# A fifth Strassen pair in the second FFN product, and a reordering of the vector work around it

## The chip, the cores and the metric

The kernel runs on one core of one Trainium2 chip. The metric is device time in microseconds (us) of one execution. Three runs of the kernel before took 1232.46, 1233.25 and 1234.97 us, so the median is 1233.25 us.

The engines are named as in the profile: PE multiplies matrices (PEld is its weight load), DVE is the vector engine, ACT the scalar engine, POOL GpSimd, and SP issues most of the DMAs. Each engine takes its instructions strictly in the order in which the program lists them for that engine; a waiting instruction holds up everything listed behind it.

## The reference, cut to what matters

The model is a two-layer trunk on 256 tokens of width 1024. Each layer is an FFN, a token mixer and a second FFN, so there are four FFN blocks in the program, and each ends in a layer norm:

```python
def _swiglu(x, w1, w3, w2):
    return (jax.nn.silu(x @ w1) * (x @ w3)) @ w2
...
for l in range(DEPTH):
    h = _swiglu(x, ffn_w1[l, 0], ffn_w3[l, 0], ffn_w2[l, 0])
    x = _layernorm(ALPHA * x + 0.5 * h, ln_g[l, 0], ln_b[l, 0])
    h = _mixer(x, l, ...)
    x = _layernorm(ALPHA * x + h, ln_g[l, 1], ln_b[l, 1])
    h = _swiglu(x, ffn_w1[l, 1], ffn_w3[l, 1], ffn_w2[l, 1])
    x = _layernorm(ALPHA * x + 0.5 * h, ln_g[l, 2], ln_b[l, 2])
```

The hidden width is 2816, so the second product `h @ w2` of each block sums over 22 slices of 128, which the kernel takes as 11 pairs of slices. Everything is float32.

## The kernel before, in words

**Split products.** PE multiplies in a reduced float32 format, so each float32 operand is cut into a high part and a low part. ACT writes the high part (a copy that rounds), then DVE writes the low part (raw minus high). One product of two blocks is three matmuls (`three`, L211): high by high, then low weight by high, then high weight by low. So the second of the three is the first that needs DVE's low split.

**Weights.** All weights stream through SBUF. A raw tile is 128 x 2048 (1 MB, one DMA from SP) out of a pool of 4; each half of it gets a high and a low tile of 128 x 1024, from pools of 8 each. `stream` (L159 to L174) does this for ordinary weights: names `raw`, `whi`, `wlo`.

**The second FFN product** (from L638 in `ffn`) is where the change lies. Eight PSUM banks of 128 x 512 hold 2 token halves t by 2 column halves c, in two sets.

- A *Strassen pair* (`SQ`, `stream_s`, names `raw`, `shi`, `slo`) multiplies its 2 x 2 blocks with seven products instead of eight: 7 x 3 = 21 matmuls of 128x512. The seven go to the banks S1 to S7 in the order 1, 2, 5, 6, 3, 7, 4. For the weight sums DVE adds in place in the raw tile (L309 over 1024 columns, L311 and L312 over 512 each). The four pieces to be split are `a` (512 columns, product 1), `b` (products 3 and 2), `c` (5 and 7, after the first sum) and `d` (6 and 4, after all sums). Two Strassen pairs share one tile for their `a` pieces. On the other side, `mixed` (L573) makes the sums of the activations: three small DVE instructions and one more split.
- A *plain pair* (`PQ`, `plain_pair`) is 8 x 3 = 24 matmuls.

The order in each block is: Strassen pair 0, plain pair, Strassen pair 1, plain pair, Strassen pair 2, plain pair, Strassen pair 3, and then four plain pairs that are *held*: they are split first, and then for each (t, c) the 24 matmuls of all four run into one bank, (0,0) first, so that the norm can start on one quarter while PE works on the next. The banks that only Strassen pairs use (S1, S5, S6, S7) close with the last Strassen pair and are added into the residual `x_tok` by eight vector instructions, the *folds* (L479, L667, L668, L477), with one ACT copy (L664). The remaining banks are added by `ln.part` (L486) when their held pairs are done.

**What sets the order.** PE's order is as written. The other engines' order is worked out at build time by a scheduler from the written order, a priority per streamed chunk and its own guess of times. `behind(x)` only forbids an instruction to stand ahead of `x`. The result is fixed before the kernel runs. How the pools give out buffers is fixed then too: a split into a high tile waits until PE has read what was in it.

Of the kernel before, what the change touches and what calls it, by code (L numbers as in the profile page):

```python
# [17 lines left out]
ALU = mybir.AluOpType  # L18
# [10 lines left out]
FB = 4  # L29
NB = 5  # L30
FR = NB * FB
NS = 4
SQ = [(FB + 2 * p, FB + 2 * p + 1) for p in range(NS)]
PQ = [(k, k + 1) for k in (0, 2, *range(FB + 2 * NS, FT, 2))]
HEADS = 8
# [21 lines left out]
def trunk(ctx, tc, x, xT, w13a, w13b, w2s, w2p, wb, wqk, wa, wbr, wo, gateb, sgug, sgub, sguwT, sgubias, lam, diffg,  # L57
          lng, lnb, lngT, lnbT, cosT, sinT, out):
    nc = tc.nc
    V, A, G, PE = nc.vector, nc.scalar, nc.gpsimd, nc.tensor  # L60
# [15 lines left out]
    def name(s):  # L76
        serial[0] += 1
        return f"{s}_{serial[0]}"
# [32 lines left out]
    def step():  # L111
        chunk[0] += 1
        tc.cur_priority = chunk[0] * STEP
# [12 lines left out]
    def beat(w):  # L126

        clock[0] += w
        for task in list(tasks):
            if task[0] <= clock[0]:  # L130
                turn(task)
# [15 lines left out]
    latest, added, emptied, silu, turned_by = [None, None], [None], [None], [None], [None]  # L147

    def behind(ins):

        return tc.issue_after(ins) if ins is not None else nullcontext()

    def stream(src, width=CH, sub=HC, lent=(), after=(None, None)):

        step()
        raw = raw_pool.tile([P, CH], F32, tag="raw", name=name("raw"))
        nc.sync.dma_start(raw[:, :width], src)  # L159
        out = []  # L160
        for o in range(0, width, HC):
            if o // HC in lent:
                hi, lo = ([act.tile([P, 512], F32R, tag="slot", name=name(n)) for _ in range(2)] for n in ("lhi", "llo"))
                at = [(hi[j], lo[j]) for j in range(2)]
            else:
                hi = hi_pool.tile([P, HC], F32R, tag="hi", name=name("whi"))
                lo = lo_pool.tile([P, HC], F32R, tag="lo", name=name("wlo"))
                at = [(hi[:, p : p + sub], lo[:, p : p + sub]) for p in range(0, HC, sub)]
            for p, (h, w) in zip(range(0, HC, sub), at):
                r = raw[:, o + p : o + p + sub]  # L170
                with behind(latest[0]):
                    A.activation(h, r, AF.Copy)  # L172
                with behind(after[o // HC] or latest[1]):
                    V.tensor_tensor(out=w, in0=r, in1=h.bitcast(F32), op=ALU.subtract)  # L174
            out.append((hi, lo))
        return out
# [34 lines left out]
    def three(ps, xh, xl, w_hi, w_lo, start, stop):  # L211

        for n, (w, xx) in enumerate([(w_hi, xh), (w_lo, xh), (w_hi, xl)]):
            PE.matmul(ps, xx, w, start=start and n == 0, stop=stop and n == 2)  # L214
# [40 lines left out]
    def rows_p(ps, t, q, piece, xh, xl, c0=0, n=512, stop=False, start=False):  # L255

        for j, k in enumerate(q):
            wh, wl = (v[:, j * 512 + c0 : j * 512 + c0 + n] for v in piece)
            three(ps[:, :n], xh(k)[:, t * P : (t + 1) * P], xl(k)[:, t * P : (t + 1) * P], wh, wl,
                  start and j == 0, stop and j == 1)  # L260
        beat(n / 1024)
# [21 lines left out]
    def stream_s(src, pair):  # L283

        step()
        raw = raw_pool.tile([P, CH], F32, tag="raw", name=name("raw"))
        nc.sync.dma_start(raw, src)

        def two():
            return hi_pool.tile([P, HC], F32R, tag="hi", name=name("shi")), lo_pool.tile([P, HC], F32R, tag="lo", name=name("slo"))  # L290

        def cut(p, o, n):
            h, w = (v[:, p[2] : p[2] + n] for v in p[:2])
            r = raw[:, o : o + n]
            with behind(latest[0]):
                A.activation(h, r, AF.Copy)  # L296
            with behind(latest[1]):
                V.tensor_tensor(out=w, in0=r, in1=h.bitcast(F32), op=ALU.subtract)  # L298

        a = (*pair, 0) if pair else None  # L300
        if a is None:
            pair = two()
            a, keep = (*pair, 0), pair
        else:
            a, keep = (*pair, 512), None
        b, c, d = ((*two(), 0) for _ in range(3))
        cut(a, 0, 512)
        cut(b, 1024, 1024)
        V.tensor_tensor(out=raw[:, :1024], in0=raw[:, :1024], in1=raw[:, 512:1536], op=ALU.add)  # L309
        cut(c, 0, 1024)  # L310
        V.tensor_tensor(out=raw[:, 1024:1536], in0=raw[:, :512], in1=raw[:, 1024:1536], op=ALU.add)  # L311
        V.tensor_tensor(out=raw[:, 1536:], in0=raw[:, 1024:1536], in1=raw[:, 1536:], op=ALU.add)  # L312
        cut(d, 1024, 1024)

        def at(p, j):
            return tuple(v[:, p[2] + j * 512 : p[2] + j * 512 + 512] for v in p[:2])

        return keep, {1: at(a, 0), 3: at(b, 0), 2: at(b, 1), 5: at(c, 0), 7: at(c, 1), 6: at(d, 0), 4: at(d, 1)}
# [246 lines left out]
    def ffn(l, f, i, norm, last=False):  # L565
# [77 lines left out]
        pair, held, plain = None, [], list(PQ)  # L643

        def plain_pair(hold):
            q = plain.pop(0)
            w = stream(w2p[l, f, PQ.index(q)])
            if hold:
                held.append((q, w))
                return  # L650
            for c in range(2):
                for t in range(NT):
                    for ps, o, m in ends[t, c]:
                        rows_p(ps, t, q, w[c], hh, hl, o, m, start=q == PQ[0] and t + c == 2)

        for n, q in enumerate(SQ):
            pair, w = stream_s(w2s[l, f, n], pair)
            for b in (1, 2, 5, 6, 3, 7, 4):
                three(S[b], *s_op[q][b], *w[b], n == 0, n == NS - 1 and b in (1, 5, 6, 7))
            beat(1.75)  # L660
            if n < NS - 1:
                plain_pair(False)
        u, v = s512("u"), s512("v")
        A.activation(u, S[6], AF.Copy)  # L664
# [2 lines left out]
        V.tensor_tensor(out=u, in0=u, in1=S[1], op=ALU.add)  # L667
        V.tensor_tensor(out=v, in0=S[5], in1=u, op=ALU.subtract)  # L668
        ln.more(0, 1, v, ALU.add, ln.scale)
        ln.more(1, 1, v, ALU.add, ln.scale)  # L670
        ln.more(1, 0, u, ALU.add)
        ln.more(1, 1, S[7], ALU.add)
        while plain:
            plain_pair(True)
        for t in range(NT):
            for c in range(2):
                for ps, o, n in ends[t, c]:
# [230 lines left out]
    for l in range(DEPTH):  # L908
        norm = ffn(l, 0, 0, norm)
        norm = mixer(l, 1, norm)  # L910
        norm = ffn(l, 1, 2, norm, last=l == DEPTH - 1)
# [89 lines left out]
```

## Time and profile before

| | |
|---|---|
| median of 3 runs | 1233.25 us |
| the profiled execution | 1233.15 us, of which its span is 1231.4 us |
| PE busy | 1215.8 us, 99% of the span, 6045 matmuls |
| DVE busy | 935.2 us, 76% |
| ACT busy | 804.0 us, 65% |
| POOL busy | 87.3 us, 7% |
| DMA | 252.28 MB, mean 205 GB/s |
| first matmul of Strassen pair 0 in the four blocks | 125.98, 552.64, 733.88 and 1160.38 us |

All times are counted from the start of the span. A row of the timeline gives the start, the time from there to the end of the row, engine, line, operation, what is written and read, and how many equal instructions the row merges; brackets give idle time of the engine just ahead of it, and what ended that. The waits table gives, for an engine and a line, the total, the number and the longest of its waits for another engine. A row of the table of stretches gives the stretch, its length, PE's busy time and matmuls, the granted PE clock as a share of full speed, and DMA.

### The profile page before, as it was taken

The page shows a single profiled execution, that of the slowest core. Times are in us where ns is not written, and L with a number is a line of the kernel's source. Part 1 is how long each engine was busy: PE and PEld are TensorE (multiplying, and loading weights), DVE is VectorE, ACT ScalarE, POOL GpSimd, SP SyncE. Part 2 cuts the span into 40 slices and gives each one's busy share as a digit, 9 for nine tenths or more (in the row PEclk, how much of TensorE's full clock was granted, in tenths as well). Part 3 has the DMA queues.
Part 4 walks back from the last instruction along what each step waited for, and adds up shares of the span by engine and source line. Part 5 has one row for each costly group of instructions (what it writes and reads, how often), then busy time and mean ns, then how long its engine had stood idle before and what let it go on. Part 6 is the DMA issues. An engine that isn't in the chain of part 4 may idle for free.

```text
span 1231.4 us, 16550 instructions
## 1 busy us (share of the span) xinstructions
PE 1215.8 (99%) x6045; PEld 1022.6 (83%) x6045; DVE 935.2 (76%) x1504; ACT 804.0 (65%) x1316; POOL 87.3 (7%) x184
## 2 busy tenths in 40 slices
PE   9999999999999999999999999999999999999997
PEld 8888878888888888888788888788888888888885
DVE  6657997886587985679974779979767879657795
ACT  6677666679665565776556776467885654776760
POOL 0100000234100000000000000002440000000000
PEclk9999999999999999999999999999999999999999
DMA  8985665654744657666756756565556356668540
GB/s 316 315 260 175 236 238 175 212 173 161 258 173 151 239 178 249 202 176 227 251 176 234 209 184 239 205 216 189 177 185 226 138 190 222 224 198 240 172 173 35
DMA packets 82338, 252.28 MB, mean 205 GB/s; under 512 B 47521, under 2 KB 48593, under 8 KB 55633
## 3 DMA queue, kind: packets, MB, share of 16 engines
q1 hardware_dynamic: 78288, 238.31, 57.5%
q0 software_dynamic: 3536, 12.13, 3.0%
q8 instruction: 47, 0.77, 0.2%
q10 hardware_dynamic: 432, 0.79, 0.2%
q14 instruction: 35, 0.28, 0.1%
HBM read 235.47 MB, written 1.05 MB: 192 GB/s over the span
## 4 chain that ended last, share of the span: by engine, by line
PE 58%; issue 22%; DVE 12%; ACT 5%; DMA 2%; POOL 1%; DVEq 0%; ACTq 0%; POOLq 0%
PE bank L214 19%; PE sbank L214 16%; PE bank L226 12%; PE bank L233 6%; DVE wlo L174 3%; DVE slo L298 3%; PE bank L385 2%; ACT shi L296 1%; ACT columns L601 1%; PE sbank L734 1%; DVE xtok L479 1%; ACT whi L172 1%; DVE raw L312 1%; DMA bc<-in_lng 1%; DVE hlo L180 1%
## 5 line engine op out<-in xcount | busy, mean ns | idle before, releaser
L174 DVE TENSOR_TENSOR wlo<-raw,whi 128x1024 fp32r<-128x1024 f32 (+1 forms) x410 | 450.7, 1117 | 161.6 <-ACT whi L172 118.0
L172 ACT ACTIVATE whi<-raw 128x1024 fp32r<-128x1024 f32 (+1 forms) x410 | 387.0, 968 | 192.5 <-PE sbank L214 67.9
L214 PE MATMUL bank<-whi,x 128*128 128x512 f32 x840 | 264.7, 391 | 0.0
L214 PEld LDWEIGHTS bank<-whi,x 128*128 128x128 f32 x840 | 157.8, 188 | 32.5
L214 PE MATMUL bank<-wlo,x 128*128 128x512 f32 x420 | 163.6, 390 | 0.0
L214 PE MATMUL sbank<-whi,x 128*128 128x512 f32 x512 | 158.9, 389 | 0.0
L226 PE MATMUL bank<-x,whi 128*128 128x512 f32 x640 | 158.4, 396 | 0.0
L226 PEld LDWEIGHTS bank<-x,whi 128*128 128x128 f32 x640 | 116.6, 188 | 25.9 <-issue 2.6
L214 PEld LDWEIGHTS sbank<-whi,x 128*128 128x128 f32 x512 | 96.1, 188 | 19.9
L214 PE MATMUL sbank<-wlo,x 128*128 128x512 f32 x256 | 99.7, 389 | 0.0
L296 ACT ACTIVATE shi<-raw 128x1024 fp32r<-128x1024 f32 (+1 forms) x64 | 58.9, 945 | 56.9 <-DVE raw L312 39.1
L214 PEld LDWEIGHTS bank<-wlo,x 128*128 128x128 f32 x420 | 78.9, 188 | 16.0
L298 DVE TENSOR_TENSOR slo<-raw,shi 128x1024 fp32r<-128x1024 f32 (+1 forms) x64 | 68.8, 1088 | 27.5 <-ACT shi L296 27.5
L233 PE MATMUL bank<-x,wlo 128*128 128x256 f32 x640 | 85.8, 285 | 0.0
L233 PEld LDWEIGHTS bank<-x,wlo 128*128 128x128 f32 x640 | 81.5, 191 | 2.3
L214 PE MATMUL sbank<-whi,hhi 128*128 128x512 f32 x168 | 66.4, 395 | 0.0
L214 PE MATMUL sbank<-wlo,hhi 128*128 128x512 f32 x168 | 66.2, 394 | 0.0
L214 PE MATMUL sbank<-whi,hlo 128*128 128x512 f32 x168 | 66.0, 393 | 0.0
L234 ACT ACTIVATE r<-bank 128x256 f32<-128x256 f32 x112 | 41.8, 379 | 27.6 <-PE bank L233 27.6
L552 ACT ACTIVATE xf<-sbank,ln_b,ln_g 128x128 f32<-128x128 f32 x80 | 30.0, 455 | 40.8 <-PE sbank L546 40.8
L214 PEld LDWEIGHTS sbank<-wlo,x 128*128 128x128 f32 x256 | 48.1, 188 | 10.0
L445 POOL DMA_DIRECT2D bc<-in_lng x6 | 3.2, 530 | 712.9 <-DVE bc L444 712.9
(233 smaller groups left out, 1938.7 us busy)
## 6 DMA issues: line engine op xcount, KB each, us to landing
raw<-in_w13b SPq DMA_DIRECT2D x76, 1024.0 KB, 5.4
raw<-in_w2p SPq DMA_DIRECT2D x28, 1024.0 KB, 4.9
raw<-in_wa SPq DMA_DIRECT2D x24, 1024.0 KB, 5.3
raw<-in_w2s SPq DMA_DIRECT2D x16, 1024.0 KB, 4.9
raw<-in_wb SPq DMA_DIRECT2D x16, 1024.0 KB, 4.9
raw<-in_wqk SPq DMA_DIRECT2D x16, 1024.0 KB, 4.8
raw<-in_wbr SPq DMA_DIRECT2D x16, 1024.0 KB, 4.8
raw<-in_w13a SPq DMA_DIRECT2D x8, 1024.0 KB, 4.8
```

The lines of the kernel that those rows point to most:

```text
L172: A.activation(h, r, AF.Copy)
L174: V.tensor_tensor(out=w, in0=r, in1=h.bitcast(F32), op=ALU.subtract)
L180: return a.ins, V.tensor_tensor(out=lo, in0=src, in1=hi.bitcast(F32), op=ALU.subtract).ins
L214: PE.matmul(ps, xx, w, start=start and n == 0, stop=stop and n == 2)
L226: PE.matmul(b[-1], hi[:, k * P : (k + 1) * P], xc(k), start=k == 0, stop=False)
L233: PE.matmul(b[n][:, :T], lo[:, k * P : (k + 1) * P], xc(k)[:, :T], start=False, stop=k == KT - 1)
L234: emptied[0] = A.activation(r[:, s], b[n][:, T:], AF.Copy, scale=scale).ins
L296: A.activation(h, r, AF.Copy)
L298: V.tensor_tensor(out=w, in0=r, in1=h.bitcast(F32), op=ALU.subtract)
L312: V.tensor_tensor(out=raw[:, 1536:], in0=raw[:, 1024:1536], in1=raw[:, 1536:], op=ALU.add)
L385: PE.matmul(ps[t][m], x[:, j, o + t * P : o + (t + 1) * P], y, start=k0 + j == 0 and o == 0 and y is hi, stop=k0 + j == KT - 1 and y is lo)
L552: A.activation(xf[:, s], b[:, s], AF.Identity, scale=self.gT[:, f], bias=self.bT[:, f])
```

## The change

One pair more goes through Strassen's form: `NS` is 5, so the plain pairs are six, not seven. A plain pair stands only behind Strassen pairs 0 and 1 (`n < 2`); pairs 2, 3 and 4 follow each other on PE without one between, and then come four held pairs, as many as before. In `stream_s` the two sums of 512 are written ahead of the split of piece `c`, and its low split may not stand ahead of the last sum (`cut(c, 0, 1024, last)`). At the end, the four held pairs are streamed ahead of the last three folds.

```diff
-NS = 4
+NS = 5
...
-        def cut(p, o, n):
+        def cut(p, o, n, after=None):
...
-            with behind(latest[1]):
+            with behind(after or latest[1]):
                 V.tensor_tensor(out=w, in0=r, in1=h.bitcast(F32), op=ALU.subtract)
...
         V.tensor_tensor(out=raw[:, :1024], in0=raw[:, :1024], in1=raw[:, 512:1536], op=ALU.add)
-        cut(c, 0, 1024)
         V.tensor_tensor(out=raw[:, 1024:1536], in0=raw[:, :512], in1=raw[:, 1024:1536], op=ALU.add)
-        V.tensor_tensor(out=raw[:, 1536:], in0=raw[:, 1024:1536], in1=raw[:, 1536:], op=ALU.add)
+        last = V.tensor_tensor(out=raw[:, 1536:], in0=raw[:, 1024:1536], in1=raw[:, 1536:], op=ALU.add).ins
+        cut(c, 0, 1024, last)
         cut(d, 1024, 1024)
...
-            if n < NS - 1:
+            if n < 2:
                 plain_pair(False)
...
         ln.more(0, 1, v, ALU.add, ln.scale)
+        while plain:
+            plain_pair(True)
         ln.more(1, 1, v, ALU.add, ln.scale)
         ln.more(1, 0, u, ALU.add)
         ln.more(1, 1, S[7], ALU.add)
-        while plain:
-            plain_pair(True)
```

In the changed kernel the two sums of 512 are lines L310 and L311. The first place where the order moves is DVE's queue in the first block, at the second Strassen pair, whose raw tile is `raw_1285` before and `raw_1293` now. Before:

```order
L298 TENSOR_TENSOR slo_1290<-raw_1285,shi_1289 128x1024
L180 TENSOR_TENSOR hlo_158<-qa_1077,hhi_151 128x512
L311 TENSOR_TENSOR raw_1285<-raw_1285 128x512
L312 TENSOR_TENSOR raw_1285<-raw_1285 128x512
L298 TENSOR_TENSOR slo_1292<-raw_1285,shi_1291 128x1024
```

Now:

```order
L310 TENSOR_TENSOR raw_1293<-raw_1293 128x512
L180 TENSOR_TENSOR hlo_156<-qa_1085,hhi_150 128x512
L311 TENSOR_TENSOR raw_1293<-raw_1293 128x512
L298 TENSOR_TENSOR slo_1298<-raw_1293,shi_1297 128x1024
L298 TENSOR_TENSOR slo_1300<-raw_1293,shi_1299 128x1024
```

The low split of piece `c` has moved from ahead of the sums to behind them, so that it stands between the last sum and the low split of piece `d`.

The second place is DVE's queue where the Strassen banks close, in the first block. `wlo` are the low splits of the held pairs (1519 and 1532 belong to the first half of the fourth held pair, before and now), `xtok`, `u` and `v` the folds. Before:

```order
L174 TENSOR_TENSOR wlo_1509<-raw_1506,whi_1508 128x1024
L667 TENSOR_TENSOR u_1475<-u_1475,bank_1204 128x512
L479 SCALAR_TENSOR_TENSOR xtok_144<-xtok_144,sbank_1202 128x512
L668 TENSOR_TENSOR v_1476<-bank_1206,u_1475 128x512
L477 TENSOR_TENSOR xtok_144<-xtok_144,u_1475 128x512
L479 SCALAR_TENSOR_TENSOR xtok_143<-xtok_143,v_1476 128x512
L479 SCALAR_TENSOR_TENSOR xtok_144<-xtok_144,v_1476 128x512
L174 TENSOR_TENSOR wlo_1513<-raw_1506,whi_1512 128x1024
L477 TENSOR_TENSOR xtok_144<-xtok_144,sbank_1202 128x512
L174 TENSOR_TENSOR wlo_1519<-raw_1516,whi_1518 128x1024
```

Now:

```order
L479 SCALAR_TENSOR_TENSOR xtok_144<-xtok_144,sbank_1210 128x512
L667 TENSOR_TENSOR u_1491<-u_1491,bank_1212 128x512
L174 TENSOR_TENSOR wlo_1516<-raw_1509,whi_1515 128x1024
L668 TENSOR_TENSOR v_1492<-bank_1214,u_1491 128x512
L174 TENSOR_TENSOR wlo_1522<-raw_1519,whi_1521 128x1024
L479 SCALAR_TENSOR_TENSOR xtok_143<-xtok_143,v_1492 128x512
L174 TENSOR_TENSOR wlo_1526<-raw_1519,whi_1525 128x1024
L174 TENSOR_TENSOR wlo_1532<-raw_1529,whi_1531 128x1024
L174 TENSOR_TENSOR wlo_1536<-raw_1529,whi_1535 128x1024
L479 SCALAR_TENSOR_TENSOR xtok_144<-xtok_144,v_1492 128x512
L477 TENSOR_TENSOR xtok_144<-xtok_144,u_1491 128x512
L477 TENSOR_TENSOR xtok_144<-xtok_144,sbank_1210 128x512
```

Three folds have moved behind the last low split of the held pairs, and three of the held pairs' low splits that stood further ahead have moved in between the other folds.

## Prediction

> **What bounds the kernel now.** I read the page first, then the waits of PE, then the timeline of PE, DVE and ACT in the second FFN product of the first block, and last the stretches around the last block's wait.
>
> ```profile
> span 1231.4 us, 16550 instructions
> PE 1215.8 (99%) x6045; PEld 1022.6 (83%) x6045; DVE 935.2 (76%) x1504; ACT 804.0 (65%) x1316; POOL 87.3 (7%) x184
> PE bank L214 <- DVE wlo L174: 9.0, 4, 3.2
> PE bank L214 <- DVE wlo L174: 1.9, 1, 1.9
> ```
>
> PE is the bound: 99% busy, and apart from its start and its tail its only waits are four, 9.0 us together, for a low split of a held pair. The last row is the answer for a window around one of the first three blocks; all three give it, so the last block's wait is the longest, 3.2 us. Here is the first block on PE:
>
> ```profile
> 125.98 0.40 PE L214 MATMUL bank<-shi,shh 128*128 128x512 f32 x1
> ...
> 136.21 0.39 PE L214 MATMUL bank<-shi,shh 128*128 128x512 f32 x1
> ...
> 161.37 0.39 PE L214 MATMUL bank<-whi,hhi 128*128 128x512 f32 x1
> ...
> 165.45 0.39 PE L214 MATMUL bank<-whi,hhi 128*128 128x512 f32 x1
> 167.75 0.50 PE L214 MATMUL bank<-wlo,hhi 128*128 128x512 f32 x1 [1.92 <-DVE wlo L174]
> ```
>
> From Strassen pair 0 (125.98) to Strassen pair 1 (136.21) stand 21 + 24 = 45 matmuls in 10.23 us: one every 0.2273 us, though each row says 0.39. The held pairs begin at 161.37. The 19th matmul there is the first that needs the fourth held pair's high split (165.45), the 20th needs its low split, and that waits until 167.75. What was DVE doing? (The last row is ACT's, from the same stretch.)
>
> ```profile
> 130.62 1.22 DVE L298 TENSOR_TENSOR slo<-raw,shi 128x1024 fp32r<-128x1024 f32 x1
> 131.75 0.69 DVE L180 TENSOR_TENSOR hlo<-qa,hhi 128x512 fp32r<-128x512 f32 x1
> 132.35 0.69 DVE L311 TENSOR_TENSOR raw<-raw 128x512 f32<-128x512 f32 x1
> 133.07 0.69 DVE L312 TENSOR_TENSOR raw<-raw 128x512 f32<-128x512 f32 x1
> 134.95 1.23 DVE L298 TENSOR_TENSOR slo<-raw,shi 128x1024 fp32r<-128x1024 f32 x1 [1.19 <-ACT shi L296]
> ...
> 151.83 0.69 DVE L312 TENSOR_TENSOR raw<-raw 128x512 f32<-128x512 f32 x1
> 153.73 1.23 DVE L298 TENSOR_TENSOR slo<-raw,shi 128x1024 fp32r<-128x1024 f32 x1 [1.21 <-ACT shi L296]
> 154.88 3.49 DVE L174 TENSOR_TENSOR wlo<-raw,whi 128x1024 fp32r<-128x1024 f32 x3
> 158.28 0.68 DVE L479 SCALAR_TENSOR_TENSOR xtok<-xtok,bank 128x512 f32<-128x512 f32 x1
> ...
> 163.55 1.29 DVE L479 SCALAR_TENSOR_TENSOR xtok<-xtok,v 128x512 f32<-128x512 f32 x2
> 164.75 1.22 DVE L174 TENSOR_TENSOR wlo<-raw,whi 128x1024 fp32r<-128x1024 f32 x1
> 165.88 0.68 DVE L477 TENSOR_TENSOR xtok<-xtok,sbank 128x512 f32<-128x512 f32 x1
> 166.48 2.35 DVE L174 TENSOR_TENSOR wlo<-raw,whi 128x1024 fp32r<-128x1024 f32 x2
> 152.64 1.06 ACT L296 ACTIVATE shi<-raw 128x1024 fp32r<-128x1024 f32 x1 [4.45 <-DVE raw L312]
> ```
>
> The split that PE wants starts at 166.48, and PE goes on 1.27 us later. Behind each other, DVE's instructions start 1.13 us apart for 1024 columns (154.88 to 158.28 for three) and 0.60 for 512 (165.88 to 166.48); if the second needs the first, 0.72 (132.35 to 133.07). From 130.62 to 166.48 DVE stops twice, each time behind the last sum of a Strassen pair: ACT can begin the high split of `d` only then (0.12 us after the sum's end, 152.64), needs 1.06 us, and DVE follows. So in this stretch DVE, not PE, sets the end. The waits sit in DVE's queue, and **the question is whether DVE's queue up to that split gets shorter**.
>
> **The change part by part.** *PE.* A Strassen pair in a plain pair's place saves 3 matmuls: 3 x 0.2273 = 0.68 us a block, 2.73 us over four. It counts only where PE is not waiting.
>
> *DVE, between the row at 130.62 and the wanted split.* I count by the order, which is fixed:
>
> - added by the fifth Strassen pair less the plain pair: one more split of 1024, 1.13; one of 512, 0.60; one sum of 1024, 1.13; two sums of 512, 0.72 + 0.60. Together **+4.18 us**.
> - gone: three folds, 3 x 0.60 = **-1.80 us**. Low splits of held pairs ahead of the wanted one are six before and six now; they only change places with folds.
> - gone: the two stops. A sum that starts at 133.07 frees DVE at 133.67, and the next row is at 134.95: 1.28. In the same way 151.83 + 0.60 = 152.43 to 153.73: 1.30. Together **-2.58 us**.
> - new: behind the last sum DVE now does the low split of `c`. It is free 0.60 + 1.13 = 1.73 us after that sum's start; the high split of `d` is there after 1.90 (151.83 to 153.73). So each of four such places (pairs 1 to 4) keeps a stop of about 0.17, and three places get 0.12 where an instruction stands right behind one that it needs. With 0.06 for the split at 131.75, which now waits for ACT, that is 1.1 us; before has some 0.2 us of such gaps in the same queue, so I take **+0.9 us**. I bound it by nothing at all from below and by 1.8 from above (both the stops and the gaps twice as long).
>
> Sum: 4.18 - 1.80 - 2.58 + 0.9 = **+0.7 us**. DVE reaches the wanted split not sooner but 0.7 us later, at 167.2, and PE goes on at 167.2 + 1.27 = 168.5 instead of 167.75. PE, with its 0.68 us less work, is there earlier and only waits longer: the split is wanted after 153 + 19 = 172 matmuls, 125.98 + 172 x 0.2273 = 165.1, so PE loses 3.4 us a block. This falls into two gaps, since the third held pair's low split now also comes late: it starts 0.60 + 2 x 1.13 = 2.87 us ahead of the other, at 164.3, is usable at 165.6, and is wanted at 163.7. So a gap of 1.9 us, six matmuls, a gap of 1.5 us.
>
> *Is DVE held up by others?* Three Strassen pairs in a row cost DVE 6.4 us each (3.5 x 1.13 + 1.13 + 1.32), and PE takes 21 x 0.2273 = 4.77. DVE comes into them with a lead and nearly spends it: from the last split of pair 4 to the wanted one stand seven splits (itself among them) and five folds, 7 x 1.13 + 5 x 0.60 = 10.9 us. The wanted one starts 167.2 - 125.98 = 41.2 us after the block's start, so that one starts at 30.3, is usable at 31.5, and is wanted after 142 matmuls, at 32.3. So some 0.7 us of lead is left, and PE does not stop before the held pairs. ACT's high splits wait until PE has read the old tiles; by the same count each of these is free before ACT gets there. The raw tile of the last held pair can be asked for once pair 4 is split, 31.5 us into the block; by the row below it is there 4.9 us later, ACT is done by 37.6, and DVE wants it at 41.2. The three folds behind the last split delay the first `ln.part` by about 1.9 us; PE needs the normalised rows only some ten us later, and they hide there.
>
> *The last block* is different. Its rows follow, behind that of the load: four of the timeline, then four stretches.
>
> ```profile
> raw<-in_w2p SPq DMA_DIRECT2D x28, 1024.0 KB, 4.9
> 1160.38 0.40 PE L214 MATMUL bank<-shi,shh 128*128 128x512 f32 x1
> 1169.64 1.06 ACT L464 ACTIVATE bc<-bc 128x1024 f32<-128x1024 f32 x1
> 1171.68 2.36 DVE L174 TENSOR_TENSOR wlo<-raw,whi 128x1024 fp32r<-128x1024 f32 x2 [0.89 <-ACT whi L172]
> 1203.44 0.50 PE L214 MATMUL bank<-wlo,hhi 128*128 128x512 f32 x1 [3.21 <-DVE wlo L174]
> 1201.36:1204.77 3.41, 1.33 (x6) 1.00 0.02 5
> 1204.77:1208.18 3.41, 3.41 (x10) 0.50 0.00 0
> 1225.25:1228.67 3.42, 1.66 (x5) 1.00 0.22 80
> 1228.67:1231.36 2.69, 0.00 (x0) 1.00 0.27 96
> ```
>
> ACT's scaling of the norm's weight (L464) stands ahead of a plain pair's high splits and costs DVE 0.89 us there, so PE goes on 43.06 us after the block's start, not 41.77 as in the first. In the changed order L464 stands behind these high splits, and DVE's count is the same as in the other blocks: 41.77 + 0.7 = 42.5, which is **0.5 us sooner**. And the long wait has a second price: after a stretch of 3.41 us with 1.33 us of matmuls the granted clock is 0.50 for the next 3.41 us, with 10 matmuls instead of 15. That loses half of 3.41, **1.7 us**. With the wait cut in two by six matmuls I take it as gone.
>
> The Trainium skill, "TensorE: Matmul & The Clock Gate", Part 1, says that the clock is halved after at least one idle window of about 3.4 us. This trace differs: the wait was 3.21 us and its window held 1.33 us of matmuls, and the clock fell. By the page's rule it would have stayed, this term would be nothing, and the sum would be 1.7 us higher, 1234.8.
>
> *Sum*, against the profiled execution's own 1233.15 us (median of the runs 1233.25): 3 x 0.7 - 0.5 - 1.7 = -0.1 us. **1233.0 us: no change** that a measurement of this kernel can tell (about 0.2%, 2.5 us). Without cover for the small stops (0 to 1.8 a block) it is 1229.5 to 1236.7.
>
> **The rivals.** *Faster: DVE is not the bound, and the waits go.* Then 2.73 us of matmuls, 9.0 us of waits and 1.7 us of half clock are saved: 1219.7. For it speaks that 2.58 us of stops and 1.8 us of folds do leave DVE's queue in each block; against it, that 4.18 + 0.9 us come in. Halfway, if the small stops vanish, each block ends 0.9 us sooner: 1229.4. Chance of ending below 1230.7 in either way: 0.20.
>
> *Slower: the clock falls in the split gaps.* Two gaps of 1.9 and 1.5 us stand around six matmuls (1.5 us). A stretch of 3.41 us that lies across them can hold as little as 1.5 us of matmuls. With 1.33 the clock fell; with 1.66 (1225.25 to 1228.67) it did not in the next. The point lies between, and how the stretches lie to the gaps is chance. Each fall costs 1.7 us; two give 1236.4, all four 1239.8. Chance of two or more: 0.10.
>
> *Slower: DVE's lead of 0.7 us in the three Strassen pairs is not there.* If it comes 1 us later, PE stops in pair 4, gives its tiles back later, ACT's high splits follow, and the lateness is passed on to the held pairs: 1 us a block, 1237. Chance 0.08.
>
> **How the numbers follow.** The forecast keeps 0.62, with 1231 to 1235 as its own range. The range 1229.5 to 1236.7 adds the bounds of the small stops, and so takes in the near halves of the first two rivals; what it leaves out (waits gone, three or more falls of the clock, a late DVE) I put at 0.2. Faster by over 0.2%: 0.20; within: 0.62; slower: 0.10 + 0.08 = 0.18.
>
> **What would show it.** In the changed profile: 12 matmuls fewer; PE waiting on `wlo` in eight places instead of four, some 12 us in all instead of 9.0, two in each block and 1 to 2 us each; no stop over 0.3 us of DVE behind a Strassen pair's last sum; PE back at the fourth held pair's low split 42.5 us after each block's start; no stretch of 0.50 clock late in the run. I am wrong if PE's wait per block falls below 2 us (DVE's sum is too high), if PE waits for `slo` (no lead), or if the clock falls in the first three blocks.

## The result, and the profile after

The changed kernel takes 1231.26 us (median of 19 runs, 1231.01 to 1232.25); the kernel before, beside it on the same chip, 1233.36 us (19 runs, 1231.49 to 1235.22). The ratio is 0.9983, with an interval of 0.9976 to 0.9990: 0.17% less, inside what I had called no change. The profiled execution took 1231.44 us, 1.7 us less than the one of before.

The page after, and the rows for low splits in the waits of PE and of DVE (in total, how often, the longest):

```profile
span 1229.7 us, 16592 instructions
PE 1212.5 (99%) x6033; PEld 1018.4 (83%) x6033; DVE 955.6 (78%) x1540; ACT 814.1 (66%) x1328; POOL 87.4 (7%) x184
```

```profile
PE bank L214 <- DVE wlo L174: 10.9, 8, 1.5
```

```profile
DVE slo L298 <- ACT shi L296: 13.3, 9, 2.3
```

PE has 12 matmuls fewer and waits longer: eight times and 10.9 us, where it was four times and 9.0. DVE is busy 20 us longer, but stops for a Strassen pair's high split only 9 times, where the kernel before has

```profile
DVE slo L298 <- ACT shi L296: 27.5, 21, 2.3
```

The first block of the changed kernel, on PE and then on DVE:

```profile
125.61 0.40 PE L214 MATMUL bank<-shi,shh 128*128 128x512 f32 x1
...
164.96 0.50 PE L214 MATMUL bank<-wlo,hhi 128*128 128x512 f32 x1 [1.53 <-DVE wlo L174]
...
166.22 0.39 PE L214 MATMUL bank<-whi,hhi 128*128 128x512 f32 x1
167.83 0.50 PE L214 MATMUL bank<-wlo,hhi 128*128 128x512 f32 x1 [1.22 <-DVE wlo L174]
```

```profile
129.93 0.68 DVE L310 TENSOR_TENSOR raw<-raw 128x512 f32<-128x512 f32 x1
130.65 0.69 DVE L180 TENSOR_TENSOR hlo<-qa,hhi 128x512 fp32r<-128x512 f32 x1
131.26 0.68 DVE L311 TENSOR_TENSOR raw<-raw 128x512 f32<-128x512 f32 x1
131.86 2.44 DVE L298 TENSOR_TENSOR slo<-raw,shi 128x1024 fp32r<-128x1024 f32 x2
...
154.32 2.52 DVE L298 TENSOR_TENSOR slo<-raw,shi 128x1024 fp32r<-128x1024 f32 x2
156.75 1.22 DVE L174 TENSOR_TENSOR wlo<-raw,whi 128x1024 fp32r<-128x1024 f32 x1
...
164.82 0.68 DVE L479 SCALAR_TENSOR_TENSOR xtok<-xtok,v 128x512 f32<-128x512 f32 x1
165.42 3.49 DVE L174 TENSOR_TENSOR wlo<-raw,whi 128x1024 fp32r<-128x1024 f32 x3
```

Two gaps stand where there was one, six matmuls apart: before the low split of the third held pair (164.96) and of the fourth (167.83). The fourth's split is the second of the three merged in the last row, so it starts at 165.42 + 1.13 = 166.55. PE goes on with it 167.83 - 125.61 = 42.2 us after the block's start, where it was 41.8. The other three blocks do the same; the last one's rows are

```profile
1161.44 0.40 PE L214 MATMUL bank<-shi,shh 128*128 128x512 f32 x1
...
1203.64 0.49 PE L214 MATMUL bank<-wlo,hhi 128*128 128x512 f32 x1 [1.21 <-DVE wlo L174]
```

that is 42.20 us where it was 43.06. In the stretches around the gaps (start and end, length, busy time and instructions of PE, PEld, DVE, ACT and POOL, then the granted clock and DMA) the clock stays full, in the first block and in the last:

```profile
163.03:166.44 3.41, 1.88 (x8) 1.05 (x6) 3.41 (x5) 3.04 (x4) 0.00 (x0) 1.00 0.89 296
166.44:169.85 3.41, 2.19 (x10) 1.69 (x10) 3.41 (x5) 2.31 (x5) 0.00 (x0) 1.00 0.93 305
```

```profile
1200.70:1204.12 3.42, 2.15 (x8) 1.49 (x9) 3.42 (x5) 0.00 (x0) 0.00 (x0) 1.00 0.01 2
1204.12:1207.53 3.41, 3.41 (x17) 2.78 (x16) 3.38 (x7) 0.00 (x0) 0.00 (x0) 1.00 0.02 5
```

So the account of the two profiled executions is: three blocks 0.4 us later each, the last one 0.9 sooner, 1.7 of half clock gone, and 0.4 gained ahead of the first block, where PE's matmuls are the same (125.98 against 125.61). I take this last one for chance: over all kernels below the start lies between 125.1 and 126.1, and in the two whose order up to there is that of the kernel before, at 125.69 and 125.83. 3 x 0.43 - 0.87 - 1.7 - 0.37 = -1.65, and measured was -1.71. By this account the two kernels take the same time at full clock.

### The profile page after: what moved, and what is told of

Read it like the earlier page. It is cut to its first block, busy times and chain, and to the rows that moved or that the text cites. A ratio compares the mean times of both kernels' runs of the same rounds, so it can differ in the third digit from the quotient of the medians.

```text
span 1229.7 us, 16592 instructions
## 1 busy us (share of the span) xinstructions
PE 1212.5 (99%) x6033; PEld 1018.4 (83%) x6033; DVE 955.6 (78%) x1540; ACT 814.1 (66%) x1328; POOL 87.4 (7%) x184
## 4 chain that ended last, share of the span: by engine, by line
PE 85%; DVE 10%; issue 3%; ACT 2%; DVEq 0%; ACTq 0%
PE bank L214 31%; PE sbank L214 19%; PE bank L226 17%; PE bank L233 9%; DVE slo L298 3%; DVE wlo L174 2%; PE sbank L226 2%; PE bank L385 2%; PE sbank L734 1%; DVE raw L309 1%; ACT shi L296 1%; DVE raw L311 1%; PE sbank L546 1%; ACT columns L601 1%; DVE raw L310 1%
## 5 line engine op out<-in xcount | busy, mean ns | idle before, releaser
L174 DVE TENSOR_TENSOR wlo<-raw,whi 128x1024 fp32r<-128x1024 f32 (+1 forms) x402 | 441.4, 1115 | 156.5 <-ACT whi L172 116.8
L172 ACT ACTIVATE whi<-raw 128x1024 fp32r<-128x1024 f32 (+1 forms) x402 | 379.4, 966 | 185.5 <-PE bank L214 62.1
L214 PE MATMUL bank<-whi,x 128*128 128x512 f32 x840 | 264.5, 390 | 0.0
L214 PEld LDWEIGHTS bank<-whi,x 128*128 128x128 f32 x840 | 157.7, 188 | 32.5
L214 PE MATMUL bank<-wlo,x 128*128 128x512 f32 x420 | 163.5, 389 | 0.0
L214 PE MATMUL sbank<-whi,x 128*128 128x512 f32 x512 | 158.9, 389 | 0.0
L214 PEld LDWEIGHTS sbank<-whi,x 128*128 128x128 f32 x512 | 96.1, 188 | 19.9
L296 ACT ACTIVATE shi<-raw 128x1024 fp32r<-128x1024 f32 (+1 forms) x80 | 73.4, 947 | 52.0 <-DVE raw L311 26.4
L214 PE MATMUL sbank<-wlo,x 128*128 128x512 f32 x256 | 99.6, 389 | 0.0
L298 DVE TENSOR_TENSOR slo<-raw,shi 128x1024 fp32r<-128x1024 f32 (+1 forms) x80 | 85.3, 1088 | 14.1 <-ACT shi L296 13.3
L214 PEld LDWEIGHTS bank<-wlo,x 128*128 128x128 f32 x420 | 78.9, 188 | 16.0
L234 ACT ACTIVATE r<-bank 128x256 f32<-128x256 f32 x112 | 41.8, 380 | 27.5 <-PE bank L233 27.5
L214 PE MATMUL sbank<-whi,hhi 128*128 128x512 f32 x144 | 56.4, 391 | 0.0
L214 PEld LDWEIGHTS sbank<-wlo,x 128*128 128x128 f32 x256 | 48.0, 188 | 10.0
L214 PE MATMUL sbank<-whi,hlo 128*128 128x512 f32 x144 | 56.1, 389 | 0.0
L214 PE MATMUL sbank<-wlo,hhi 128*128 128x512 f32 x144 | 56.1, 389 | 0.0
```

What stands on the lines that cost most here:

```text
L234: emptied[0] = A.activation(r[:, s], b[n][:, T:], AF.Copy, scale=scale).ins
```

## The experiments

**Theory 1**, my forecast's: DVE's queue up to the wanted split sets the end of each block, a saved matmul only becomes wait, and what the change gains is the shorter wait of the last block and the half clock. **Theory 2**: the gain is that of the 12 matmuls, and the queue's order matters little. Each run below was compared with runs of the kernel before on the same chip, whose median was between 1232.6 and 1233.3 us.

The change has three parts, and eight kernels hold each of their combinations. Six of them were new. This table comes first, since all six are read from it; the times within are of the first block.

| Strassen pairs | sums ahead | folds behind | block's start | wanted split's start | difference | PE's waits for low splits, all blocks | time |
|---|---|---|---|---|---|---|---|
| 4 | no | no (the kernel before) | 125.98 | 166.48 | 40.50 | 9.0 us, 4 | 1232.6 |
| 4 | yes | no | 125.88 | 165.60 | 39.72 | 4.5 us, 4 | 1226.9 |
| 4 | no | yes | 125.29 | 163.99 | 38.70 | 1.5 us, 1 | 1223.6 |
| 4 | yes | yes | 125.16 | 163.07 | 37.91 | none | 1221.1 |
| 5 | no | no | 125.17 | 169.38 | 44.21 | 18.8 us, 10 | 1251.5 |
| 5 | yes | no | 126.10 | 168.84 | 42.74 | 15.0 us, 6 | 1241.1 |
| 5 | no | yes | 125.26 | 167.68 | 42.42 | 12.2 us, 12 | 1240.8 |
| 5 | yes | yes (the change) | 125.61 | 166.55 | 40.94 | 10.9 us, 8 | 1231.3 |

**The fifth pair alone.**

```diff
-NS = 4
+NS = 5
-            if n < NS - 1:
+            if n < 2:
```

> The kernel before with the fifth Strassen pair alone (four held pairs streamed from n < 2, as in the change), the sums and the folds where they stood. Theory 1, DVE's queue sets the end of the second FFN product and a saved matmul only becomes wait: the added 4.18 us of DVE work and one more stop of about 1.3 us stand in each block with little taken away, so each block ends at least 3.9 us later and the longer waits let the clock fall in some blocks (1.7 us each): about 1250 us, 1245 to 1260. Theory 2, PE's matmuls are the gain and the queue's order hardly matters: 12 matmuls fewer, 2.7 us faster than the kernel before, about 1230.5.

1251.5 us, a ratio of 1.0152 (1.0138 to 1.0166): 12 matmuls fewer, and 19 us slower. Its waits, and a stretch behind a gap:

```profile
PE bank L214 <- DVE wlo L174: 17.1, 8, 3.6
PE bank L214 <- DVE slo L298: 1.7, 2, 0.9
```

```profile
167.75:174.58 6.83, 6.20 (x15) 4.85 (x16) 6.29 (x8) 2.11 (x4) 0.00 (x0) 0.50 0.95 351
```

The wanted split comes 3.71 us later, and the wait of up to 3.6 us makes the clock fall in all four blocks, for 23.9 us together, which costs up to 12 us more. In the last block PE even waits inside the Strassen pairs (`slo`). Theory 2 is out for this part.

**The sums alone.**

```diff
-        cut(c, 0, 1024)
         V.tensor_tensor(out=raw[:, 1024:1536], in0=raw[:, :512], in1=raw[:, 1024:1536], op=ALU.add)
-        V.tensor_tensor(out=raw[:, 1536:], in0=raw[:, 1024:1536], in1=raw[:, 1536:], op=ALU.add)
+        last = V.tensor_tensor(out=raw[:, 1536:], in0=raw[:, 1024:1536], in1=raw[:, 1536:], op=ALU.add).ins
+        cut(c, 0, 1024, last)
```

> The kernel before with the sums of a Strassen piece ahead of the low split of c, and nothing else; 6045 matmuls as before. Theory 1: the two stops of DVE (2.58 us a block) go, small ones of about 0.4 come, but the folds ahead of the wanted split then wait for PE's bank instead of DVE being late, so PE goes on only about 0.8 us a block sooner (41.0 us after the block's start instead of 41.77), 2.1 in the last block, and its half clock of 1.7 us goes: about 1227. Theory 2: no matmul is saved, so no change, 1233.

1226.89 us, 0.9951 (0.9939 to 0.9964). As theory 1 had it (about 1227). The two stops are worth 2.6 us a block, but the wanted split comes only 0.78 us sooner, because DVE now arrives early at a fold whose bank PE has not closed:

```profile
157.39 0.69 DVE L479 SCALAR_TENSOR_TENSOR xtok<-xtok,bank 128x512 f32<-128x512 f32 x1 [1.03 <-PE bank L214]
```

**The folds alone.**

```diff
+        while plain:
+            plain_pair(True)
         ln.more(1, 1, v, ALU.add, ln.scale)
         ln.more(1, 0, u, ALU.add)
         ln.more(1, 1, S[7], ALU.add)
-        while plain:
-            plain_pair(True)
```

> The kernel before with three of the folds behind the held pairs' splits, and nothing else; 6045 matmuls. Theory 1: three folds of 0.60 us go from ahead of the wanted split, so PE goes on 1.8 us sooner (40.0 us after the block's start instead of 41.77), waits some 0.3 us instead of 2, and the half clock goes: 4 x 1.8 + 1.7 = 8.9 us faster, about 1224.3. Theory 2: no matmul is saved, so no change, 1233.

1223.58 us, 0.9926 (0.9914 to 0.9939). The wanted split comes 1.80 us sooner, three folds of 0.60. One wait for a low split is left in the whole run, 1.5 us in the last block, where L464 still delays DVE. Theory 1.

**Both orders, four pairs.** The two diffs above together.

> The kernel before with both orders of the change, sums ahead and three folds behind, and still four Strassen pairs: no matmul is saved. Theory 1, DVE's queue was the bound of each block's end and the change spends the room that the orders give on the fifth Strassen pair: all waits for low splits go, the last block's too, 9.0 us of them and 1.7 of half clock: about 1222. Theory 2, the gain of the change comes from its 12 matmuls: no gain without them, 1233.

1221.06 us, 0.9900 (0.9886 to 0.9913). This is the fastest kernel of the study, 12 us under the kernel before and 10 under the changed one, with no matmul saved. Its list of PE's waits has no low split in it; all of it is

```profile
PE sbank L397 <- DVE warm L393: 1.0, 1, 1.0
PE sbank L514 <- DVE xtok L493: 1.0, 1, 1.0
PE bank L385 <- ACT whi L179: 0.6, 1, 0.6
PE sbank L518 <- ACT minus L516: 0.2, 1, 0.2
```

Theory 1: the room on DVE that the two orders make was worth 12 us, and the fifth pair spends 10 of them.

**Five pairs, the sums without the folds.** The changed kernel with the folds' diff undone.

> The changed kernel with its three folds put back ahead of the held pairs' splits. Theory 1: 1.8 us more on DVE ahead of the wanted split in each block, 4 x 1.8 = 7.2 above the changed kernel's 1231.3, so about 1238.5, and up to 1245 if the longer waits let the clock fall in each block. Theory 2: as the changed kernel, 1231.

1241.13 us, 1.0070 (1.0057 to 1.0083). The wanted split comes 1.80 us later than in the changed kernel, as three folds of 0.60 say; and in its profile the clock falls in all four blocks. Theory 1.

**Five pairs, the folds without the sums.** The changed kernel with the sums' diff undone.

> The changed kernel with the sums put back behind the low split of c. Theory 1: DVE's two to three stops of 1.3 us stand again, but with three folds fewer ahead of the wanted split PE goes on about 41.4 us after a block's start (43.2 in the kernel with five pairs alone, less 1.8), 0.8 sooner than in the changed kernel, and some 42.8 in the last block (44.6 less 1.8), 0.6 later: 1231.3 - 3 x 0.8 + 0.6 = about 1229.5, and 1.7 more for each fall of the clock. That would mean that the change's sums cost it time. Theory 2: as the changed kernel, 1231. Theory 3, the stops add up as in my forecast's sum: 2.58 - 0.9 = 1.7 us a block more than the changed kernel, about 1238.

1240.80 us, 1.0063 (1.0049 to 1.0076). Theory 1 as I wrote it there missed by 11 us, and theory 3 came nearest. The miss was one of reading: I took the gap at 43.2 us of the first experiment for the fourth held pair's, and it was the third's. The fourth's split was usable at 45.5, but PE, at half clock, had only just come to it, so no gap showed. From the table, the sums are worth 1.47 us a block with five pairs, near the 1.7 that my forecast's terms give (2.58 less 0.9).

**A gap filled with matmuls.** The kernel before, with 9 matmuls whose result nothing reads, in the last block's wait.

```diff
+                        if last and t + c == 0 and q == held[-1][0]:
+                            for _ in range(3):
+                                three(S[6], hh(PQ[0][0])[:, :P], hl(PQ[0][0])[:, :P], *(x[:, :512] for x in held[0][1][0]), True, True)
```

> The kernel before with 9 matmuls more, whose result nothing reads, on TensorE alone and in the last block alone, put where it waits for the low split of the fourth held pair; DVE's and ACT's work and order as before. Theory 1, the long wait itself makes the clock fall and the fall costs 1.7 us: the 9 matmuls (2.05 us) lie inside the wait of 3.2 us, no stretch of 0.50 clock follows, and the time is 1.7 us shorter than the kernel before in those of its runs in which its clock fell: about 1231.5, with a smaller spread. Theory 2, the half clock costs nothing at the end or has another cause: 1233, with the same spread.

1231.14 us, 0.9990 (0.9981 to 0.9999). PE is back at the wanted split as late as before (43.17 us after the block's start), and the stretch behind it runs at full clock, with 17 matmuls instead of 10:

```profile
1200.67:1204.08 3.41, 2.13 (x10) 1.46 (x9) 3.41 (x4) 0.00 (x0) 0.00 (x0) 1.00 0.00 0
1204.08:1207.49 3.41, 3.41 (x17) 2.79 (x16) 1.62 (x4) 0.00 (x0) 0.00 (x0) 1.00 0.00 0
```

More matmuls on the busiest engine, and a slightly faster kernel: the half clock is a price of the gap. The spread became smaller, 1.8 us against 3.3, but did not go. Seven of 11 runs stand at 1230.7 to 1231.4 and four at 1232.3 to 1232.5, which fits a fall in one of the first three blocks, whose waits were left as they were; the profile is of a run without one.

**Matmuls taken away, all else as before.** The kernel before without one of the seven products of the last Strassen pair.

```diff
-            for b in (1, 2, 5, 6, 3, 7, 4):
+            for b in (1, 2, 5, 6, 3, 7, 4)[: 6 if n == 3 else 7]:
```

> The kernel before with one of the seven products (three matmuls) of the last Strassen pair left out in each block: 12 matmuls fewer, as in the change, and every other engine's order word for word as before. Its output lacks these products. Theory 1, a matmul saved ahead of the held pairs only lengthens the wait: PE goes on 41.8 us after each block's start as before, waits 2.6 us instead of 1.9, and gains nothing; since more of the wait falls into one stretch of 3.41 us, the clock falls more often: no faster, 1232.5 to 1237. Theory 2, the matmuls are the gain: 2.7 us faster, about 1230.

1236.66 us, 1.0024 (1.0011 to 1.0038): 12 matmuls fewer and slower. In the first block, which starts at 125.83, PE is back 41.80 us later, as in the kernel before, and has waited 2.62 us instead of 1.92:

```profile
167.63 0.80 PE L214 MATMUL bank<-wlo,hhi 128*128 128x512 f32 x1 [2.62 <-DVE wlo L174]
```

```profile
163.54:166.96 3.42, 1.47 (x7) 0.89 (x5) 3.42 (x5) 2.75 (x6) 0.00 (x0) 1.00 0.30 101
166.96:170.37 3.41, 2.74 (x7) 2.17 (x8) 2.55 (x4) 0.00 (x0) 0.00 (x0) 0.50 1.02 324
```

The saved 0.68 us went whole into the wait, the longer wait emptied a stretch, and the clock fell; in this profile in every block, 17.1 us in all. Its single runs stand about 1.7 us or twice that apart, near 1233.2, 1234.9, 1238.4 and 1240.2, as whole falls would put them. This rules out theory 2.

**Could five pairs gain, with all folds behind?** The changed kernel with the streaming of the held pairs ahead of all eight folds.

```diff
+        while plain:
+            plain_pair(True)
         ln.more(1, 0, S[7], ALU.subtract, ln.scale)
...
-        while plain:
-            plain_pair(True)
         ln.more(1, 1, v, ALU.add, ln.scale)
```

> The changed kernel with the streaming of the held pairs written ahead of all the folds, so that every low split of a held pair stands ahead of every fold in DVE's queue. Theory 1: five folds more leave DVE's queue ahead of the wanted split, 5 x 0.60 = 3.0 us; PE goes on at 39.2 us after a block's start, when it wants it at 39.1, the waits go and the 12 saved matmuls count at last: 1231.3 - 4 x 3.0 = about 1219, faster than both kernels. Theory 2, PE is the bound already: 1231. Theory 3, the folds that now come late hold the banks of the Strassen products or the next half's tiles: some new wait of PE for DVE's folds, 1222 to 1231.

1224.12 us, 0.9927 (0.9914 to 0.9939): 7 us under the changed kernel, but 3 above four pairs with both orders. The waits for low splits are gone but for 0.4 us, and others have come, at the transposes of the normalised rows (L546), in three blocks:

```profile
PE sbank L546 <- DVE xtok L502: 2.8, 2, 1.4
PE sbank L546 <- issue: 1.4, 1, 1.4
PE bank L214 <- DVE wlo L174: 0.4, 1, 0.4
```

Here are the ends of the norm's chain on DVE, between its statistics (L498) and the normalised rows (L502), first in this kernel and then in the one with four pairs and both orders:

```profile
174.05 0.20 DVE L498 BATCH_NORM_AGGREGATE mv<-st 128x2 f32<-128x12 f32 x1
...
179.15 1.00 DVE L502 TENSOR_SCALAR xtok<-xtok,mv,nwy 128x512 f32<-128x512 f32 x2
```

```profile
173.55 0.21 DVE L498 BATCH_NORM_AGGREGATE mv<-st 128x2 f32<-128x12 f32 x1
...
175.85 1.00 DVE L502 TENSOR_SCALAR xtok<-xtok,mv,nwy 128x512 f32<-128x512 f32 x2
```

5.1 us against 2.3. With five pairs DVE has not yet split the next weights when the norm begins, and four of these splits, with an addition and the statistics of the second half, stand between the chain's small steps. From the first block's start to the second's it takes 425.85 us, with four pairs 424.28. Of theory 1 the first part came, since the waits for low splits went; the time lies in theory 3's range, but what PE waits for is the norm and not a fold.

**The second half's folds behind the first half's norm.** As the last kernel, with the four folds into t = 1 written behind the norm of t = 0 and kept behind its last instruction.

```diff
+            if t == 0:
+                with behind(ln.ends[0]):
+                    ln.more(1, 0, S[7], ALU.subtract, ln.scale)
+                    ln.more(1, 0, u, ALU.add)
+                    ln.more(1, 1, v, ALU.add, ln.scale)
+                    ln.more(1, 1, S[7], ALU.add)
```

> The changed kernel with the streaming of the held pairs ahead of all folds, and the four folds into the second half of the rows (t = 1) moved behind the normalised rows of the first half. Theory 1: DVE reaches the norm of the first half 2.4 us sooner than in the run with all folds behind, so TensorE's wait of 1.8 us for the transposes in three blocks goes too, and the 12 saved matmuls count: 1224.1 - 3 x 1.8 = about 1218.7, 2.4 under the kernel with four pairs and both orders (1221.06). Theory 2, DVE is full up to that place whatever the order: about 1224. Theory 3, the folds that now come later delay the second half's norm or the next splits: 1221 or more.

1224.84 us, 0.9931 (0.9918 to 0.9943). The wait of the first half's transposes went, and the same wait stands at the second half's, 66.2 to 66.6 us into a block instead of 54.3 to 54.7:

```profile
PE sbank L546 <- DVE xtok L502: 4.2, 3, 1.4
```

The 1.8 us of my text, here and in the next one, was the first block's two waits together (1.4 and 0.4); the wait for the transposes is 1.4. The work was only moved. Theory 2: in each of these orders DVE is late by the same amount somewhere ahead of the next stage.

**Two folds on GpSimd.** The kernel with all folds behind, with the folds of `u` and `v` into t = 1 as GpSimd additions.

```diff
-        ln.more(1, 1, v, ALU.add, ln.scale)
-        ln.more(1, 0, u, ALU.add)
-        ln.more(1, 1, S[7], ALU.add)
+        ln.more(1, 1, S[7], ALU.add, ln.scale)
+        for c, w in ((0, u), (1, v)):
+            y = ln.y[1][:, c * 512 : (c + 1) * 512]
+            G.tensor_tensor(out=y, in0=y, in1=w, op=ALU.add)
```

> The changed kernel with all folds behind the held pairs' splits, and two of the folds into the second half of the rows (of u and of v) done by GpSimd instead of VectorE: 1.2 us of DVE's work less in each block. Theory 1, with five Strassen pairs DVE's work, in whatever order, is the bound from the block's start to the next transposes: the wait of 1.8 us there shrinks by 1.2 in three blocks: 1224.1 - 3.6 = about 1220.5. Theory 2, the wait there has another cause than DVE's load (GpSimd's or ACT's latency in the norm): 1224. Theory 3, GpSimd's adds (1.6 us each in the rotary rows) come late for the second half's norm: 1222 to 1226.

1223.10 us, 0.9914 (0.9900 to 0.9928): 1.0 us less than with the folds on DVE, not 3.6. GpSimd's additions and DVE beside them:

```profile
168.74 1.29 POOL L675 TENSOR_TENSOR xtok<-xtok,u 128x512 f32<-128x512 f32 x1 [37.14 <-DVE u L669]
170.00 1.28 POOL L675 TENSOR_TENSOR xtok<-xtok,v 128x512 f32<-128x512 f32 x1
```

```profile
169.77 0.68 DVE L486 TENSOR_TENSOR xtok<-xtok,bank 128x512 f32<-128x512 f32 x1
170.37 1.47 DVE L479 SCALAR_TENSOR_TENSOR xtok<-xtok,v 128x512 f32<-128x512 f32 x1
```

The fold at 170.37 takes 1.47 us beside GpSimd's second addition, where the same fold takes 0.68 elsewhere. It is the same in the other three blocks (1.53, 1.53 and 1.54 us). So of the 1.2 us taken off DVE some 0.8 came back. PE's wait for the transposes fell from 1.4 to 0.9 us in each of three blocks, not by 1.2. Taking work off DVE helps, as theory 1 has it, but by much less than its share of DVE's queue. Whether the splits between the norm's steps are what costs five pairs the last 1.4 us a block was read from the trace; a kernel with them moved away was not tried.

## Why the prediction was right, and where not

- **DVE, not PE, is the bound there.** Shown from both sides: 12 matmuls taken away gain nothing (1236.66), and three folds moved gain 9 us (1223.58). Both of the change's gaps are where I put them, 2.87 us apart, behind the two splits that I named; each is 0.3 to 0.4 us shorter than I said (1.53 and 1.22 us).
- **+0.7 us a block: the count is right, its start is not.** From DVE's first row behind the two copies of L444 to the wanted split it takes 166.48 - 130.62 = 35.86 us before and 166.55 - 129.93 = 36.62 us in the changed kernel: +0.76. So the sum holds, the small stops too: 4.18 - 1.80 - 2.58 + x = 0.76 gives x = 0.96, where I had 0.9. But counted from the block's start on PE the wanted split is only 40.94 - 40.50 = 0.44 us later. What I had put at nothing, without a reason, is where that first row stands: 4.32 us after the block's start, not 4.64. The same order of the sums acts on Strassen pair 0 too, which is split ahead of the block's start. The first two rows are of before, the third of the changed kernel:

```profile
119.61 1.06 ACT L296 ACTIVATE shi<-raw 128x1024 fp32r<-128x1024 f32 x1 [2.07 <-DVE raw L312]
124.76 0.76 DVE L236 TENSOR_TENSOR silu<-sbank,r 128x256 f32<-128x256 f32 x2 [0.18 <-ACT r L234]
117.73 1.06 ACT L296 ACTIVATE shi<-raw 128x1024 fp32r<-128x1024 f32 x1 [0.54 <-DVE raw L311]
```

ACT waits 2.07 us for DVE's last sum before, 0.54 now, and DVE no longer waits for ACT at L236. With the sums alone the first row stands at 4.37, with the folds alone at 4.64, so it comes with the sums. From the experiments the 0.44 is +3.71 for the pair, -1.47 for the sums and -1.80 for the folds, the last as I had it. From the last Strassen split to the wanted one it is 10.9 us in the text and in the trace.

- **Last block: -0.5, measured -0.87.** The step is right, L464 no longer delays it and the block ends as the others do (42.2 us); the rest is the same earlier start of DVE's queue.
- **Half clock: -1.7, as said.** No fall in this profile until PE's work is done. But I took the fall as a fixed price of the last block. The runs speak for a matter of chance in each block with a long gap: those of before spread over 3.7 us, those of the change over 1.2.
- **Lead in the three Strassen pairs.** PE waits for no `slo`, so this rival and its 4 us fall away. Without the sums it is real in the last block: the first experiment has two such waits there.
- **Where the 1.6 us between -0.1 and -1.7 lie:** three times 0.27 and 0.37 in the last block, from the earlier start of DVE's queue, and 0.37 ahead of the first block, which I could not have had.
- **The faster rival** ("the waits go") did not come, for the reason given: 4.18 us came into DVE's queue.

What I did not see is what the parts were worth apart. I weighed them as one sum near zero; taken apart they are -12 and +10 us. The sum in my own text said so (-1.80 and -2.58 against +4.18 a block), and I did not ask what the kernel would do with the negative terms alone.

## What to carry to other kernels

If a change joins a saving on the busiest engine to a relief of the engine that it waits for, work out each by itself: here the relief alone was worth 12 us and the fifth pair alone cost 19, though PE was 99% busy. Ask at each stage which engine ends the wait, and count a fewer-multiplications form by what it adds there. And look at how long PE's gaps are, not only at their sum: a gap that empties one stretch of the clock's watch costs another 1.7 us.

## What the runs showed of the hardware

**When the clock falls.** The prediction had it between 1.33 and 1.66 us of matmuls in a stretch of 3.41. The runs draw the line closer. Two kernels, five pairs with the folds and then the one with matmuls taken away:

```profile
162.34:165.75 3.41, 1.71 (x7) 1.05 (x6) 3.41 (x5) 2.38 (x3) 0.00 (x0) 1.00 0.70 286
...
776.75:780.16 3.41, 1.61 (x7) 1.01 (x6) 3.41 (x5) 2.68 (x5) 0.00 (x0) 1.00 0.74 233
780.16:783.57 3.41, 3.22 (x8) 2.10 (x7) 3.41 (x5) 1.39 (x3) 0.00 (x0) 0.50 1.00 370
```

```profile
1204.61:1208.02 3.41, 1.63 (x8) 1.00 (x6) 3.41 (x6) 0.00 (x0) 0.00 (x0) 1.00 0.00 0
1208.02:1211.43 3.41, 1.07 (x5) 0.88 (x6) 3.41 (x4) 0.00 (x0) 0.00 (x0) 1.00 0.00 0
1211.43:1214.85 3.42, 3.42 (x10) 2.65 (x9) 1.45 (x4) 0.00 (x0) 0.00 (x0) 0.50 0.02 5
```

Behind 1.61 us the clock was halved, behind 1.63 and 1.71 it was not, and the changed kernel's emptiest stretch around its gaps held 1.88. So a fall needs no idle stretch: among the matmuls of this product a stretch some 47% busy lay at the line, and a gap of 1.8 us was enough where it lay whole in one. It is no share that holds for all matmuls. In the run's tail PE does others (L514 and L518, 512 ns each in the mean, where those of L214 take 390), and there the kernel with the folds alone kept its clock behind less:

```profile
1216.03:1219.44 3.41, 1.43 (x4) 0.55 (x4) 1.96 (x5) 0.00 (x0) 0.00 (x0) 1.00 0.33 121
```

The prediction's 1.66 us stood in that tail too. Where the stretches lie to the gaps differs between the profiled executions, which would explain the spread of the kernel before. The Trainium skill, "TensorE: Matmul & The Clock Gate", Part 1, calls the window 3413 ns and free-running, which agrees with the stretches of 3.41 us here; its idle window as the condition does not agree.

**GpSimd beside DVE.** A fold of 0.68 us took 1.47 to 1.54 us, in all four blocks, while GpSimd added two tiles of SBUF. The Trainium skill, "GPSIMD Engine Reference", Specifications, says that GpSimd contends with vector instructions that have two SBUF inputs; the fold of `v` is one, and the row agrees. The addition ahead of it (L486), whose second input is a bank, kept its 0.68.
